# A two-layer encoder on one core: order of the activation sums behind the norm's row, order of the weight sums ahead of their split, sizes of two small tiles

## The chip, the cores and the metric

One NeuronCore of a Trainium2 chip runs the whole network. The time is device microseconds of one execution, the median of several. A profile of one execution lists every instruction of the five engines (TensorE for matmuls, VectorE and ScalarE for elementwise work, GpSimd, and SyncE, which issues the loads) with its start, its duration and what it waited for.

## The reference

Two layers over 256 tokens of width 2048, in float32. Layer 0 mixes with pooling and grouped-query attention, layer 1 with an mLSTM matrix memory. After each mixer comes a gated feed-forward, which is where this change acts:

```python
def conv_ffn(x, w_up, conv_w, conv_b, w_down):
    u = x @ w_up
    up = jnp.pad(u, ((0, 0), (1, 1), (0, 0)))
    c = conv_w.astype(u.dtype)
    u = c[0] * up[:, :-2] + c[1] * up[:, 1:-1] + c[2] * up[:, 2:] + conv_b.astype(u.dtype)
    gate, val = jnp.split(u, 2, axis=-1)
    return (jax.nn.silu(gate) * val) @ w_down
...
        x = x + mixed
        x = x + conv_ffn(rms_norm(x, norm_ffn[layer]), w_up[layer], conv_w[layer], conv_b[layer], w_down[layer])
```

The width of the gate and of the value is 5632 each. `rms_norm` divides each token's row by its root mean square and multiplies by a gain per column.

## The kernel before

**Products in two parts.** Float32 weights and activations are split into a high part of a shorter format and the remainder; a product is high x high + high x low + low x high, three passes through TensorE. The activations after a norm are the tile `xx` (high and low), scaled by the gain but not by the token's factor, which is multiplied on after the matmul.

**The stream of weights.** All weights come in chunks of 128 x 1024 float32, 512 KB, in the order of their use. `Stream.load` (L81) lets SyncE load a chunk into a `w` buffer (six, and one more in the feed-forward, from the pool `fw`). `Stream.split` (L93) makes the high part on ScalarE (L105) and the remainder on VectorE (L106) into an `hl` buffer (four, and one more in the feed-forward, from the pool `fh`). `Stream.next` (L120) hands the chunk to the matmuls after keeping loads up to seven and splits up to three chunks ahead, in the feed-forward. Some chunks carry a `kind`: for "sum" the right half gets the left half added (L99); for "chain" the left half first gets the right half of the last "sum" chunk added (L102), and then the right half gets the left (L103). A "sum" chunk's buffer is thus read until the "chain" chunk that follows it has been added.

**The feed-forward.** `_ffn_plan` writes out the order of steps: six groups of 4 or 8 column tiles; `up` computes a tile of gate and of value from 4 chunks, `down` multiplies finished groups by `w_down`. In two groups, four tiles are computed by `quads` instead: a block product with seven instead of eight multiplications, which needs sums of blocks of the activations (`sx`, made by `sums`, L930) and of the weights (the "sum" and "chain" chunks). `UNITS` says between which groups of the plan the chunks of a quad are strewn; there are 28 chunks for each of two quads in each of two layers. Each quad makes seven products `p` per pair of blocks; the first half of `sx` serves the first four pairs, the second half the last four.

**The row of the norm.** `Norm.finish` (L294) adds up the squares (L298), takes the inverse root (`rsqrt`, L224 to L231, with one power on GpSimd, L226) and gets a column `rcol` of factors. For norms 1 and 3, the ones ahead of the feed-forwards, it then makes two diagonal matrices `dg` (L310), multiplies them by ones on TensorE (tile `npr`, L313), and copies the product out as the row R (L315). `n0` (L1085) is minus `rcol`.

**What sets the order.** TensorE runs in the order of the program. The program itself is woven: generators such as `Norm.finish`, `sums_ready` and `quads`' `finish` are queued with a delay in estimated microseconds (`Weave.add`), and each step of the stream of matmuls advances that clock (`Weave.tick`) and lets at most one task go on. `Weave.until` runs tasks until something is there; the first `up` asks with it for R (L925). Within this order, the instructions of VectorE, ScalarE, GpSimd and SyncE are put in order by a list scheduler that plays the program through with estimated durations and takes, when an engine is free, the earliest instruction of the program that is ready. It can therefore put an instruction far ahead of its place in the program. On the chip each engine then works strictly in the order so found. `tc.keep_in_program_order(ins)` adds an edge, for order alone, from the last instruction traced on the same engine before `ins`: the scheduler may not put `ins` ahead of that one.

Of the kernel before, what the change touches and what calls it, by code (L numbers as in the profile page):

```python
# [9 lines left out]
F32 = mybir.dt.float32  # L10
# [6 lines left out]
P = 128  # L17
# [47 lines left out]
class Stream:  # L65


    def __init__(self, nc, wpool, spool, srcs, load_ahead, split_ahead):
        self.nc, self.wpool, self.spool, self.srcs = nc, wpool, spool, srcs
        self.la, self.sa = load_ahead, split_ahead  # L70
        self.w, self.hl = {}, {}
        self.n_load = self.n_split = self.at = 0
        self.more = None
# [7 lines left out]
    def load(self, pieces=1):  # L81
        i = self.n_load
        src = self.srcs[i]
        kind, src = src if isinstance(src, tuple) else ("plain", src)
        width = src.shape[-1]
        n = width // pieces
        w = self.home(i, True).tile([P, CH * P], F32, tag="w", name=f"w{i}")
        for c in range(0, width, n):
            self.nc.sync.dma_start(w[:, c : c + n], src[:, c : c + n])
        self.w[i] = w, n, width, kind  # L90
        self.n_load += 1

    def split(self, then=None):  # L93
        i = self.n_split
        w, n, width, kind = self.w.pop(i)
        hl = self.home(i, False).tile([P, 2, CH * P], F32R, tag="hl", name=f"hl{i}")
        l, r = w[:, 0:512], w[:, 512:1024]
        if kind == "sum":
            self.nc.vector.tensor_add(r, r, l)  # L99
            self.sum = r  # L100
        if kind == "chain":
            self.nc.vector.tensor_add(l, l, self.sum)  # L102
            self.nc.vector.tensor_add(r, r, l)  # L103
        for c in range(0, width, n):
            (self.nc.vector.tensor_copy if i + c == 0 else self.nc.scalar.copy)(hl[:, 0, c : c + n], w[:, c : c + n])  # L105
            self.nc.vector.tensor_sub(hl[:, 1, c : c + n], w[:, c : c + n], hl[:, 0, c : c + n].bitcast(F32))  # L106
            then and then(c // n)
        self.hl[i] = hl
        self.n_split += 1

    def ahead(self, i, split=None):
        n = len(self.srcs)
# [14 lines left out]
class Weave:  # L127
# [6 lines left out]
    def add(self, gen, delay=0.0):  # L134
        self.q.append([self.t + delay, gen])
# [37 lines left out]
def trunk(ctx: ExitStack, tc: tile.TileContext, gx, xT, xn, call, catt, cml, weights, out):  # L173
    nc = tc.nc
    v, a, g, pe = nc.vector, nc.scalar, nc.gpsimd, nc.tensor
# [7 lines left out]
    wp = pool("wraw", 6)  # L183
    sp = pool("wsplit", 4)
    smp = pool("small", 2)
    sm1 = pool("small1", 1)
# [5 lines left out]
    gcol = cp.tile([P, NG], F32, tag="gcol", name="gcol")  # L192
    a_x = actp.tile([P, KT, S], F32, tag="B1", name="xT")
    x = xp.tile([P, 2, D], F32, tag="x", name="x")
    st = Stream(nc, wp, sp, weights, 5, 2)

    gx0 = actp.tile([P, NG + 2 * S], F32, tag="B0", name="gx0")
    ctx.enter_context(tc.manual_schedule(engines={mybir.EngineType.PE}))
# [11 lines left out]
    wv = Weave()  # L210
# [34 lines left out]
    class Norm:  # L245
# [48 lines left out]
        def finish(self):  # L294
            n = self.n
            yield from wv.wait(lambda: self.blocks == NB)
            s2 = smp.tile([P, 2], F32, tag="nsum", name=f"nsum{n}")
            v.tensor_reduce(s2, self.ss, AX.X, ALU.add)  # L298
            self.rcol = rsqrt(s2, 2, 1.0 / D, f"n{n}")
            yield 2.5  # L300
            if n % 2 == 0:
                rr = dram.tile([2, P], F32, tag="rr", name=f"rr{n}")
                g.dma_start(rr.rearrange("t p -> p t"), self.rcol)
                R = sm1.tile([P, S], F32, tag="R", name=f"R{n}")
                g.dma_start(R.rearrange("p (t q) -> p t q", t=2), rr.unsqueeze(0).to_broadcast([P, 2, P]))
                self.R = R
                return
            dg = sm1.tile([P, 2, P], F32, tag="dg", name=f"dg{n}")
            for t in range(2):
                v.tensor_scalar_mul(dg[:, t, :], ident, self.rcol[:, t : t + 1])  # L310
            yield 1.0
            pr = psp.tile([P, 512], F32, tag="ps", name=f"npr{n}")
            mm(pr[:, 0:S], ones, dg.rearrange("p a b -> p (a b)"), True, True)  # L313
            R = sm1.tile([P, S], F32, tag="R", name=f"R{n}")
            v.tensor_copy(R, pr[:, 0:S])  # L315
            self.R = R
# [571 lines left out]
    def ffn_layer(layer, norm, nxt):  # L888
        with ExitStack() as es:
# [4 lines left out]
            xsp = cp1 = lp(f"fs{layer}", 1)  # L894
# [35 lines left out]
            def sums():  # L930

                vv = actp.tile([P, 2, KT // 2, S], F32, tag="B1", name=f"v{layer}")
                for h in range(2):
                    ks = slice(8 * h, 8 * h + 8)
                    v.tensor_add(vv[:, 0], norm.xx[:, ks, 0, :].bitcast(F32), norm.xx[:, ks, 1, :].bitcast(F32))
                    yield 5.0
                    q = vv[:, 0].rearrange("p (a k) (t c) -> p a k t c", k=2, t=2)
                    a11, a21, a12, a22 = (q[:, :, k, t, :] for k in range(2) for t in range(2))
                    raw = vv[:, 1].rearrange("p k s -> p (k s)").rearrange("p (j a c) -> p j a c", j=4, a=4)
                    s1, s2, s3, s4 = (raw[:, j] for j in range(4))  # L940
                    v.tensor_sub(s1, a21, a22)
                    v.tensor_add(s3, a11, a21)
                    yield 3.0
                    v.scalar_tensor_tensor(s2, s1, -1.0, a11, ALU.mult, ALU.subtract)
                    v.tensor_sub(s4, s3, a12)
                    v.tensor_sub(s4, s4, a22)
                    yield 4.0
                    for j in range(4):
                        hi, lo = (sx[:, j, 4 * h : 4 * h + 4, i, :] for i in range(2))
                        a.copy(hi, raw[:, j])  # L950
                        v.tensor_sub(lo, raw[:, j], hi.bitcast(F32))
                        yield 2.0
# [15 lines left out]
            def quads(fs, gt, i0, name):  # L968
# [8 lines left out]
                r0, r1 = norm.rcol[:, 0:1], norm.rcol[:, 1:2]  # L977
                for p in range(m):
                    ends = p == 0, p == m - 1
                    hl = st.next()  # L980
                    if p == 0:
                        b1, b5 = bank(1), bank(5)
                    product(b1, block_of(2 * p, 0), hl, 0, *ends)
                    product(b5, sum_of(0, p), hl, 512, *ends)
                    yield
                    hl = st.next()
                    if p == 0:
                        b6, b4 = bank(6), bank(4)
                    product(b6, sum_of(1, p), hl, 0, *ends)
                    product(b4, block_of(2 * p + 1, 1), hl, 512, *ends)  # L990
                    if p == m - 1:
                        c12, c21, c22 = part(12), part(21), part(22)
                        a.activation(c12, b1, AF.Copy, scale=n0)
                        a.activation(c21, b1, AF.Copy, scale=r1)
                        a.activation(c22, b5, AF.Copy, scale=r1)
                        v.scalar_tensor_tensor(c12, b6, n0, c12, ALU.mult, ALU.add)
                    yield
# [21 lines left out]
            def finish(top, bottom, fs, gt, i0, name):  # L1019

                for n, f in enumerate(fs):
                    tr = psp.tile([P, 2, S], F32, tag="ps", name=f"tr{layer}_{f}")
                    for j in range(2):
                        for t, src in enumerate((top, bottom)):
                            c = (2 * j + n) * P
                            pe.transpose(tr[:, j, t * P : t * P + P], src[:, c : c + P], ident)
                    u = tp.tile([P, 2, S], F32, tag="tb", name=f"tb_{layer}_{f}")
                    a.copy(u, tr)
                    tail(u, f, gt, i0 + n)
                    yield 2.5  # L1030

            def down_end(gt, b, kts):

# [44 lines left out]
            wv.add(norm.finish(), 4.0)  # L1078
            sx = xsp.tile([P, 4, KT // 2, 2, P], F32R, tag="sx", name=f"sx{layer}")

            n0 = xsp.tile([P, 1], F32, tag="n0", name=f"n0_{layer}")

            def sums_ready():
                yield from wv.wait(lambda: norm.R is not None)
                v.tensor_scalar_mul(n0, norm.rcol[:, 0:1], -1.0)  # L1085
                yield from sums()

            wv.add(sums_ready(), 8.0)
            st.la, st.sa, st.more = 7, 3, (lp(f"fw{layer}", 1), lp(f"fh{layer}", 1), st.at + len(_ffn_plan()))
            gts, run = {}, {}  # L1090
            for step in _ffn_plan():
                kind, c = step[:2]
                if kind != "d" and c not in gts:
# [78 lines left out]
    return np.concatenate(out)  # L1172


UNITS = {2: (1, 3), 4: (3, 5)}


def _ffn_plan():

    slots, begin = [], []  # L1180
# [9 lines left out]
    begin.append(len(slots))  # L1190
    here = [[] for _ in slots]
    m = KT // 2
    for c, (c0, c1) in UNITS.items():
        lo, hi = begin[c0] + 2, begin[c1] - 7
        one, two = 2 * m, m + m // 2
        step = (hi - lo - 3) / (one + two)
        for k in range(one + two):
            here[int(lo + k * step + (3 if k >= one else 0))].append(("s", c, 0))
# [148 lines left out]
```

## Time and profile before

| | us |
|---|---|
| median of 3 runs | 2224.29 |
| runs | 2223.16, 2224.29, 2226.46 |
| the profiled execution | 2224.29 |
| its span, first to last instruction | 2222.0 |
| TensorE busy | 2193.0 |
| VectorE busy | 1668.8 |
| ScalarE busy | 1228.3 |
| mean granted TensorE clock | 0.995 of full |

A row of the profile names a line of the kernel, an engine, an operation, the tile that it writes and those that it reads (`hl<-w,hl`), the form, and how often it occurs. "PE" is TensorE's matmuls, "PEld" its weight loads, "DVE" VectorE, "ACT" ScalarE, "POOL" GpSimd, "SPq" SyncE's queue of loads. What follows `<-` in square brackets is what ended the idle time before the instruction. The line L219 is a helper that issues all matmuls, so that they are told apart by their tiles: `up` and `dn` of the feed-forward, `p` of the quads, `npr` of the norm's row. In the timeline, instructions of one kind that follow each other are merged into one row.

### The profile page before, as it was taken

The page shows a single profiled execution, that of the slowest core. Times are in us where ns is not written, and L with a number is a line of the kernel's source. Part 1 is how long each engine was busy: PE and PEld are TensorE (multiplying, and loading weights), DVE is VectorE, ACT ScalarE, POOL GpSimd, SP SyncE. Part 2 cuts the span into 40 slices and gives each one's busy share as a digit, 9 for nine tenths or more (in the row PEclk, how much of TensorE's full clock was granted, in tenths as well). Part 3 has the DMA queues.
Part 4 walks back from the last instruction along what each step waited for, and adds up shares of the span by engine and source line. Part 5 has one row for each costly group of instructions (what it writes and reads, how often), then busy time and mean ns, then how long its engine had stood idle before and what let it go on. Part 6 is the DMA issues. An engine that isn't in the chain of part 4 may idle for free.

```text
span 2222.0 us, 30399 instructions
## 1 busy us (share of the span) xinstructions
PE 2193.0 (99%) x11328; PEld 1864.8 (84%) x11328; DVE 1668.8 (75%) x2378; ACT 1228.3 (55%) x1744; POOL 28.1 (1%) x40
## 2 busy tenths in 40 slices
PE   9999899999999999999999999989999999999999
PEld 7888688888888888889888888868888888888887
DVE  7686778788787787666767666677878878778764
ACT  7675555556555565556555455545555655556552
POOL 0020000000000000000000000000000000000000
PEclk9999999999999999999999999999999999999999
DMA  8545546676666766556555555645667666676553
GB/s 317 187 157 181 170 164 215 209 239 215 217 221 222 222 198 191 188 157 206 163 193 184 185 180 167 198 162 165 213 210 238 217 215 220 223 223 199 190 190 123
DMA packets 124951, 440.88 MB, mean 198 GB/s; under 512 B 13851, under 2 KB 16195, under 8 KB 124803
## 3 DMA queue, kind: packets, MB, share of 16 engines
q1 hardware_dynamic: 121568, 434.93, 59.8%
q10 hardware_dynamic: 3074, 3.75, 0.7%
q8 instruction: 89, 1.46, 0.3%
q0 software_dynamic: 160, 0.26, 0.1%
q14 instruction: 60, 0.48, 0.1%
HBM read 436.74 MB, written 2.14 MB: 198 GB/s over the span
## 4 chain that ended last, share of the span: by engine, by line
PE 85%; DVE 6%; DMA 6%; issue 2%; ACT 0%; DVEq 0%; ACTq 0%
PE up L219 27%; PE dn L219 20%; PE op L219 8%; DMA w<-in_q 6%; PE p L219 5%; PE mv L219 4%; PE mq L219 4%; PE mk L219 4%; PE mo L219 4%; DVE hl L106 3%; PE qproj L219 3%; PE kproj L219 1%; PE pool L219 1%; PE vproj L219 1%; PE qk L219 1%
## 5 line engine op out<-in xcount | busy, mean ns | idle before, releaser
L106 DVE TENSOR_TENSOR hl<-w,hl 128x1024 fp32r<-128x1024 f32 (+1 forms) x820 | 992.3, 1217 | 295.8 <-ACT hl L105 291.7
L105 ACT CAST hl<-w 128x1024 fp32r<-128x1024 f32 (+1 forms) x819 | 851.7, 1047 | 570.6 <-PE up L219 185.5
L219 PE MATMUL up<-xx,hl 128*128 128x512 f32 (+1 forms) x4608 | 829.7, 338 | 1.9 <-DVE hl L106 1.9
L219 PEld LDWEIGHTS up<-xx,hl 128*128 128x128 f32 x4608 | 719.5, 189 | 114.6 <-DVE hl L106 4.8
L219 PE MATMUL dn<-hl,g 128*128 128x512 f32 x2064 | 485.0, 391 | 0.6 <-DVE hl L106 0.6
L219 PEld LDWEIGHTS dn<-hl,g 128*128 128x128 f32 x2064 | 385.2, 188 | 83.2 <-DVE hl L106 1.2
L908 ACT ACTIVATE y<-tb_up,cst 128x256 f32<-128x256 f32 x144 | 78.8, 595 | 84.6 <-DVE tb_up L927 83.5
L219 PE MATMUL p<-hl,sx 128*128 128x512 f32 x384 | 104.2, 393 | 0.0
L99 DVE TENSOR_TENSOR w<-w 128x512 f32<-128x512 f32 x64 | 44.3, 692 | 76.4 <-DMA w<-in_q 76.2
L382 ACT COPY tb_up<-up 128x512 f32<-128x512 f32 x72 | 42.2, 586 | 102.6 <-PE up L219 100.3
L219 PE MATMUL mk<-xx,hl 128*128 128x512 f32 (+1 forms) x512 | 92.2, 337 | 0.0
L219 PE MATMUL mq<-xx,hl 128*128 128x512 f32 (+1 forms) x512 | 92.1, 337 | 0.0
L219 PE MATMUL mv<-hl,xx 128*128 128x512 f32 (+2 forms) x480 | 91.7, 350 | 0.0
L219 PE MATMUL op<-hl,cat 128*128 128x512 f32 x384 | 91.6, 393 | 0.0
L219 PE MATMUL mo<-hl,xx 128*128 128x512 f32 x384 | 90.4, 391 | 0.0
L219 PE MATMUL op<-hl,mcat 128*128 128x512 f32 x384 | 89.5, 392 | 0.0
L219 PEld LDWEIGHTS mq<-xx,hl 128*128 128x128 f32 x512 | 79.2, 188 | 11.6
L219 PEld LDWEIGHTS mk<-xx,hl 128*128 128x128 f32 x512 | 79.0, 188 | 11.4
L219 PEld LDWEIGHTS mv<-hl,xx 128*128 128x128 f32 x480 | 78.3, 189 | 11.2
L219 PEld LDWEIGHTS op<-hl,mcat 128*128 128x128 f32 x384 | 71.5, 188 | 14.6
L219 PEld LDWEIGHTS mo<-hl,xx 128*128 128x128 f32 x384 | 71.0, 188 | 14.1
L219 PEld LDWEIGHTS op<-hl,cat 128*128 128x128 f32 x384 | 70.9, 188 | 14.1
(240 smaller groups left out, 1746.9 us busy)
## 6 DMA issues: line engine op xcount, KB each, us to landing
w<-in_up SPq DMA_DIRECT2D x288, 512.0 KB, 4.1
w<-in_dn SPq DMA_DIRECT2D x176, 512.0 KB, 4.3
w<-in_m_in SPq DMA_DIRECT2D x124, 512.0 KB, 4.1
w<-in_q SPq DMA_DIRECT2D x112, 512.0 KB, 4.2
w<-in_a_in SPq DMA_DIRECT2D x46, 512.0 KB, 4.3
w<-in_a_out SPq DMA_DIRECT2D x32, 512.0 KB, 3.4
w<-in_m_out SPq DMA_DIRECT2D x32, 512.0 KB, 3.5
w<-in_m_g SPq DMA_DIRECT2D x5, 432.0 KB, 3.5
```

The lines of the kernel that those rows point to most:

```text
L99: self.nc.vector.tensor_add(r, r, l)
L105: (self.nc.vector.tensor_copy if i + c == 0 else self.nc.scalar.copy)(hl[:, 0, c : c + n], w[:, c : c + n])
L106: self.nc.vector.tensor_sub(hl[:, 1, c : c + n], w[:, c : c + n], hl[:, 0, c : c + n].bitcast(F32))
L219: pe.matmul(out_, lhsT, rhs, start=start, stop=stop, skip_group_check=True)
L382: a.copy(tb, ps[:, :, 1, :])
L908: a.activation(y[:, j, :], u[:, j, :], AF.Identity, scale=cw(tl, 1), bias=cw(tl, 3))
```

## The change

The sums of activations (L935, in each of two halves) and the sums of weights are pinned with `keep_in_program_order`. The weight sums move out of `split` into a function `sums`, called for chunk i + 1 at the end of the split of chunk i (and for chunk i at the start of its own, if that hasn't happened). The task that makes the activation sums is queued with a delay of 14 instead of 8. The tiles `dg` and `n0` are allocated larger, which puts the feed-forward's pools on multiples of 256 bytes. A second quad of a layer now asks that the first's `finish` tasks be done (`late`). `UNITS` spells out offsets that were written in `_ffn_plan`, with the same values.

```diff
-        self.w[i] = w, n, width, kind
+        self.w[i] = [w, n, width, kind, False]
         self.n_load += 1
+
+    def sums(self, i):
+        if i in self.w and not self.w[i][4] and self.w[i][3] != "plain":
+            w, kind = self.w[i][0], self.w[i][3]
+            l, r = w[:, 0:512], w[:, 512:1024]
+            pin, add = self.tc.keep_in_program_order, self.nc.vector.tensor_add
+            if kind == "sum":
+                pin(add(r, r, l))
+                self.sum = r
+            if kind == "chain":
+                pin(add(l, l, self.sum))
+                pin(add(r, r, l))
+            self.w[i][4] = True
 
     def split(self, then=None):
         i = self.n_split
-        w, n, width, kind = self.w.pop(i)
+        self.sums(i)
+        w, n, width = self.w.pop(i)[:3]
         hl = self.home(i, False).tile([P, 2, CH * P], F32R, tag="hl", name=f"hl{i}")
-        l, r = w[:, 0:512], w[:, 512:1024]
-        if kind == "sum":
-            self.nc.vector.tensor_add(r, r, l)
-            self.sum = r
-        if kind == "chain":
-            self.nc.vector.tensor_add(l, l, self.sum)
-            self.nc.vector.tensor_add(r, r, l)
...
         self.hl[i] = hl
         self.n_split += 1
+        self.sums(i + 1)
...
-            dg = sm1.tile([P, 2, P], F32, tag="dg", name=f"dg{n}")
+            dg = sm1.tile([P, 2 * P + 16], F32, tag="dg", name=f"dg{n}")[:, : 2 * P]
+            dg = dg.rearrange("p (t q) -> p t q", t=2)
...
-                    v.tensor_add(vv[:, 0], norm.xx[:, ks, 0, :].bitcast(F32), norm.xx[:, ks, 1, :].bitcast(F32))
+                    tc.keep_in_program_order(
+                        v.tensor_add(vv[:, 0], norm.xx[:, ks, 0, :].bitcast(F32), norm.xx[:, ks, 1, :].bitcast(F32)))
...
+                    if p == 0:
+                        wv.until(lambda: not late)
+                        late.update((0, 2))
...
+                late.discard((i0 - 4) % 4)
...
-            n0 = xsp.tile([P, 1], F32, tag="n0", name=f"n0_{layer}")
+            n0 = xsp.tile([P, 64], F32, tag="n0", name=f"n0_{layer}")[:, 0:1]
...
-            wv.add(sums_ready(), 8.0)
+            wv.add(sums_ready(), 14.0)
...
-UNITS = {2: (1, 3), 4: (3, 5)}
+UNITS = {2: (1, 2, 3, -7), 4: (3, 2, 5, -7)}
...
-    for c, (c0, c1) in UNITS.items():
-        lo, hi = begin[c0] + 2, begin[c1] - 7
+    for c, (c0, d0, c1, d1) in UNITS.items():
+        lo, hi = begin[c0] + d0, begin[c1] + d1
```

More of the change, by code (lines that the diff above doesn't have):

```diff
@@ L65, with __init__ @@
 class Stream:
-    def __init__(self, nc, wpool, spool, srcs, load_ahead, split_ahead):
-        self.nc, self.wpool, self.spool, self.srcs = nc, wpool, spool, srcs
+    def __init__(self, tc, wpool, spool, srcs, load_ahead, split_ahead):
+        self.tc, self.nc, self.wpool, self.spool, self.srcs = tc, tc.nc, wpool, spool, srcs
         self.la, self.sa = load_ahead, split_ahead
@@ L194, in trunk @@
     x = xp.tile([P, 2, D], F32, tag="x", name="x")
-    st = Stream(nc, wp, sp, weights, 5, 2)
+    st = Stream(tc, wp, sp, weights, 5, 2)
     gx0 = actp.tile([P, NG + 2 * S], F32, tag="B0", name="gx0")
@@ L1086, in sums_ready @@
                 yield from sums()
-            wv.add(sums_ready(), 8.0)
+            wv.add(sums_ready(), 14.0)
             st.la, st.sa, st.more = 7, 3, (lp(f"fw{layer}", 1), lp(f"fh{layer}", 1), st.at + len(_ffn_plan()))
-            gts, run = {}, {}
+            gts, run, late = {}, {}, set()
             for step in _ffn_plan():
```

## The prediction

> **What bounds the kernel now.** I read the page's first line and busy shares first.
>
> ```profile
> span 2222.0 us, 30399 instructions
> ...
> PE 2193.0 (99%) x11328; PEld 1864.8 (84%) x11328; DVE 1668.8 (75%) x2378; ACT 1228.3 (55%) x1744; POOL 28.1 (1%) x40
> ```
>
> TensorE is busy 2193.0 of 2222.0 us. No matmul is added or removed, so the change can win only TensorE's idle time, about 29 us, and time in which its matmuls run slower than elsewhere. What ends the idle time is in the view of waits, for matmuls (PE) and weight loads (PEld): total us, number, longest.
>
> ```profile
> PE npr L219 <- DVE n L1085: 21.3, 2, 10.7
> ...
> PEld up L219 <- DVE hl L106: 4.8, 7, 1.2
> PEld dn L219 <- DVE hl L106: 1.2, 2, 0.7
> ```
>
> Nearly all of it is two waits of 10.7 us, one in each feed-forward, for the matmul `npr` that spreads the norm's factors into the row R. The name L1085 (n0) is an accident of order: it ends beside `dg` (L310), which `npr` reads. The rest are small waits for a split chunk (L106), 6.0 us at the weight loads. In the timeline (start, us, what) VectorE around the first of the two, a cast of ScalarE, then TensorE:
>
> ```profile
> 257.18 2.28 DVE L935 TENSOR_TENSOR v<-xx 128x2048 f32<-128x2048 f32 x1
> 259.38 1.22 DVE L106 TENSOR_TENSOR hl<-w,hl 128x1024 fp32r<-128x1024 f32 x1
> 260.52 0.15 DVE L298 TENSOR_REDUCE nsum<-nss 128x2 f32<-128x8 f32 x1
> ...
> 270.59 2.29 DVE L935 TENSOR_TENSOR v<-xx 128x2048 f32<-128x2048 f32 x1
> 272.79 0.68 DVE L951 TENSOR_TENSOR sx<-v,sx 128x512 fp32r<-128x512 f32 x1
> 273.39 0.16 DVE L230 TENSOR_SCALAR re_n<-re_n 128x2 f32<-128x2 f32 x1
> ...
> 275.94 0.48 DVE L310 TENSOR_SCALAR dg<-cst,re_n 128x128 f32<-128x128 f32 x2
> ...
> 265.24 1.05 ACT L105 CAST hl<-w 128x1024 fp32r<-128x1024 f32 x1
> ...
> 260.76 5.14 PE L219 MATMUL up<-xx,hl 128*128 128x512 f32 x28
> 276.56 1.19 PE L219 MATMUL npr<-dg,cst 128*128 128x256 f32 x2 [10.66 <-DVE n L1085]
> ```
>
> The norm's chain is six instructions of 0.15 us on VectorE (L298, L224, L228 to L231), one on GpSimd and two for `dg`, yet L298 to L310 takes 15.4 us: into each gap the scheduler has put a piece of the activation sums (L935 to L951), which could run as soon as their blocks of xx were there. TensorE is through at 260.76 + 5.14 = 265.90 and stands until 276.56.
>
> **Part 1, L935 pinned behind n0.** n0 reads the norm's factor, so L935, and with it every later step of the sums, moves behind the chain. Each L935 gives back 2.2 us (270.59 to 272.79, start to next start), each 512-wide piece 0.6 (272.79 to 273.39). Ahead of `dg` stand two L935 and 13 such pieces (L941, L942, L944 and L945 twice, L946 once, L951 four times): 2 x 2.2 + 13 x 0.6 = 12.2 us. Without them `dg` starts at 275.94 - 12.2 = 263.7 and `npr` could go at 264.3, before TensorE needs it at 265.9. What could still hold it is a split: two L106 of 1.22 us let in ahead of `dg` make `npr` 266.7, a stall of 0.8. The worst that I see is the split of the cast at 265.24: it is ready at 266.3, ends at 267.5, then come L229 to L231, `dg` and the 0.6 from `dg` to `npr`, 269.2 in all, a stall of 3.3. So the two stalls of 21.3 leave between 0 and 6.6. I take 0.5 each, nearer to the sum that ends 1.6 us early: **-20.3**.
>
> What runs after the stall is slower too. Windows of TensorE: width, busy, granted clock, DMA share, GB/s; then TensorE's timeline.
>
> ```profile
> 277.00:281.00 4.00, 4.00 (x14) 0.53 0.00 0
> ...
> 1497.00:1501.00 4.00, 4.00 (x12) 0.50 0.00 0
> 1501.00:1505.00 4.00, 4.00 (x21) 0.79 0.00 0
> ...
> 277.19 45.91 PE L219 MATMUL up<-xx,hl 128*128 128x512 f32 x252
> 322.94 0.87 PE L219 MATMUL p<-hl,xx 128*128 128x512 f32 x3
> ...
> 851.70 22.46 PE L219 MATMUL up<-xx,hl 128*128 128x512 f32 x128
> 873.99 11.12 PE L219 MATMUL dn<-hl,g 128*128 128x512 f32 x48
> ...
> 1497.47 46.65 PE L219 MATMUL up<-xx,hl 128*128 128x512 f32 x252
> 1543.96 0.86 PE L219 MATMUL p<-hl,xx 128*128 128x512 f32 x3
> ```
>
> The granted clock is 0.53 and 0.50 in the 4 us after the stalls. In a stretch with no disturbance 128 matmuls of `up` take 873.99 - 851.70 = 22.29, 174.1 ns each; 252 should take 43.9. After the stalls they took 45.75 and 46.49: 1.9 and 2.6 lost. With no stall: **-4.5**; with one long enough to bring the clock down: 0.
>
> The Trainium skill, page "TensorE: Matmul & The Clock Gate", section "Part 1: The HAM clock gate (the "warmup" mystery)", says that an idle window of about 3.4 us halves TensorE's clock, and that as much sustained work restores it. The trace agrees: 0.53 and 0.50, full again some 4 to 8 us later. By that rule a stall merely cut to 4 us would keep the whole 4.5; by the row alone the loss could shrink with the stall.
>
> **Part 2, what the sums now collide with.** They are not gone. By line and form (count, busy us, mean ns), both feed-forwards together:
>
> ```profile
> L951 DVE TENSOR_TENSOR sx<-v,sx 128x512 fp32r<-128x512 f32 x16 | 10.6, 680 | 0.0
> L935 DVE TENSOR_TENSOR v<-xx 128x2048 f32<-128x2048 f32 x4 | 9.1, 2283 | 0.0
> L945 DVE TENSOR_TENSOR v<-v 128x512 f32<-128x512 f32 x4 | 2.7, 683 | 0.0
> ...
> 256.00:277.00 21.00, 10.34 (x61) 9.04 (x60) 21.00 (x36) 11.36 (x19) 0.71 (x1) 0.85 0.38 127
> 277.00:323.00 46.00, 46.00 (x255) 39.99 (x255) 36.40 (x55) 26.09 (x36) 0.00 (x0) 0.96 0.47 157
> ...
> 323.00:534.00 211.00, 172.43 (x228) 1.00 0.67 222
> ...
> 323.00:534.00 211.00, 107.18 (x91) 1.00 0.67 222
> ```
>
> Five lines like L945 make 13.5, so 33.2 in all, 16.6 us a layer. The windows give PE, PEld, DVE, ACT, POOL; the third DVE alone, the last L106 alone (91 splits in 211 us, one in 2.3). VectorE works 21.00 + 36.40 = 57.4 us between 256 and 323, and without stall and clock loss that stretch shrinks from 67 to 54.4. It cannot hold everything. But the first product with a sum comes at its end, and the half of the sums that it needs (8.3 us) fits: 57.4 - 8.3 = 49.1 of 54.4. The other half is read from the ninth quad chunk on, some 60 us later, where VectorE has 211 - 172.4 = 38.6 us free. I take **0**. The bound if the free time can't be used, since VectorE works in order: 16.6 less the 46 - 36.4 = 9.6 that are free in the first stretch, 7 us a layer, 14 in all. ScalarE's casts of the sums (L950) move along; it is half idle in both windows. Moving the task's start from 8 to 14 only lowers its rank behind the splits. What stands behind a delayed L935 is the copy of R (L315), which the first tail needs only after the first `up` group; so 0.
>
> **Part 3, weight sums one chunk ahead of their split.** The count stays (64 of L99, 32 each of L102 and L103). The groups of these adds by line (count, busy us, mean ns, idle before and what ended it), the page's row of these loads (count, size, us to landing), and the place where it hurts most:
>
> ```profile
> L99 DVE TENSOR_TENSOR w<-w 128x512 f32<-128x512 f32 x64 | 44.3, 692 | 76.4 <-DMA w<-in_q 76.2
> ...
> L102 DVE TENSOR_TENSOR w<-w,w 128x512 f32<-128x512 f32 x32 | 22.1, 691 | 36.2 <-DMA w<-in_q 35.9
> ...
> w<-in_q SPq DMA_DIRECT2D x112, 512.0 KB, 4.2
> ...
> 1619.54 0.33 SPq L89 DMA_DIRECT2D w<-in_q  x1
> 1623.78 0.69 DVE L102 TENSOR_TENSOR w<-w,w 128x512 f32<-128x512 f32 x1 [3.13 <-DMA w<-in_q]
> 1625.59 1.22 DVE L106 TENSOR_TENSOR hl<-w,hl 128x1024 fp32r<-128x1024 f32 x1
> ...
> 1626.86 5.39 PE L219 MATMUL up<-xx,hl 128*128 128x256 f32 x30 [0.81 <-DVE hl L106]
> ```
>
> VectorE stood 76.2 + 35.9 = 112 us for chunks that hadn't landed; behind the one at 1623.78 waited the split that TensorE wanted. Pinned behind the split of the chunk before it, a sum meets data loaded several splits earlier, and these waits end. That can win at most the 6.0 us at the weight loads; 0 if other VectorE work makes the same splits late. I take two thirds, as the worst of them is of this kind: **-4**. The new cost: ScalarE's cast of a quad chunk now starts after VectorE's previous split and the sum, so VectorE can wait for that cast: 1.05 us at each of 112 / 4 = 28 quad chunks of a stretch, 29.4 us, with the 8.3 from part 2 37.7 of the 38.6 free if no tail is put into the holes. Tight, but 0; what goes beyond is in rival (b). SyncE: the w buffer of a "sum" chunk is held until the "chain" chunk's add, some two splits longer than now, and SyncE's queue stands behind it; loads are issued seven buffers ahead, so 0, and the price without that lead is the slower rival.
>
> **Part 4, the rest.** Rounding `dg` and `n0` up shifts the feed-forward's buffers; splits in them now take what others take, and nothing is timed by a load's landing: 0, bounds -1 and +1. `UNITS` spells out the same starts and ends; `late` waits for transposes that are traced long before the second quads begin: 0.
>
> **The sum.** The profiled execution took 2224.29 us (2.3 around its span) and is itself the median of the three. 2224.3 - 20.3 - 4.5 - 4 = **2195.5**; with the bounds on the good side (21.3, 4.5, 6.0, 1) 2191.5.
>
> **Rivals.**
> (a) *The row still comes late.* Splits and L285 fill the gaps of the chain instead of the sums; 3.3 us remain at each, the clock still falls: 14.7 + 0 + 4 = 18.7, **2205.6**. For it: four L106 stood in that window. Against: they come up at TensorE's pace, not all at once.
> (b) *VectorE becomes the bound.* The 14 us of part 2 are paid, at the first products: **2209.5**. For it: 100% busy in the first window, and 37.7 of 38.6 above. Against: over half of that, 12.2, is the sums themselves, and 112 us of waits are freed.
> (c) *Slower: loads come late.* Where a chain chunk's add holds the sum chunk's buffer, SyncE's queue stands, and the held loads land after TensorE has used up its split chunks. The longest wait of TensorE for a split is now 1.2 us; at each of the 32 chain chunks (L102) that is 38.4, against 20.3 + 4.5 won: 2224.3 + 13.6 = **2237.9**. It decides once the lead of a load falls below the 4.2 us to landing plus cast and split, 6.5 us; seven buffers of 2.3 us less two leave 11.5.
> (d) *It doesn't do what it says.* L935 is ordered only behind n0; if pieces of the chain other than the sums set its pace, nothing but part 3 is won: **2220.3**.
>
> **How the numbers follow.** Forecast 0.66 (2190 to 2201, from the bounds), (a) 0.13, (b) 0.11, (c) 0.06, (d) 0.04. The range 2190 to 2211 holds the forecast and rivals (a) and (b), so leaves out 0.10 and the tails of these. A measurement tells about 0.2%, 4.4 us, from no change: faster 0.90, same 0.04, slower 0.06.
>
> **What would show it.** No row "npr <- DVE" of over 1 us; L935 after L1085 in time; granted clock 1.00 in the first 50 us of each feed-forward and 252 matmuls of `up` in 43.9 us; no "w <- DMA w<-in_q" among VectorE's waits; PEld's "hl L106" under 2 us. It is wrong if TensorE waits for `sx`, if "hl L106" grows past 10 us, or if SyncE's loads of the quads land after the cast that wants them.

## The result, and the profile after

| | before | after |
|---|---|---|
| median of the runs side by side, us | 2225.38 (2223.16 to 2227.27) | 2188.64 (2188.49 to 2188.67) |
| ratio, with 95% interval | | 0.9838 (0.9824 to 0.9851) |
| span of the profiled execution, us | 2222.0 | 2186.3 |

Faster, as forecast, but by more: 2188.64 against 2195.5, and below the range's low end of 2190. The profiled spans differ by 35.7 us; the forecast was 28.8. First the page's head, then two views of the changed kernel: the waits of TensorE and its weight loads for splits, with VectorE's longest (total us, number, longest), and the timeline of VectorE and TensorE around the norm's row of layer 0. The lines of the kernel have moved on: L113 is the split, L945 the first step of the activation sums, L1099 `n0`, L319 `dg`, L227 the helper of the matmuls.

```profile
span 2186.3 us, 30347 instructions
...
PE 2180.1 (100%) x11328; PEld 1861.1 (85%) x11328; DVE 1673.3 (77%) x2378; ACT 1229.4 (56%) x1744; POOL 29.2 (1%) x40
```

```profile
DVE hl L113 <- ACT hl L112: 350.8, 340, 2.6
...
PEld p L227 <- DVE hl L113: 1.7, 2, 0.8
...
PE p L227 <- DVE hl L113: 1.1, 2, 0.5
```

```profile
258.60 0.16 DVE L306 TENSOR_REDUCE nsum<-nss 128x2 f32<-128x8 f32 x1
...
259.99 1.23 DVE L113 TENSOR_TENSOR hl<-w,hl 128x1024 fp32r<-128x1024 f32 x1
...
262.63 0.47 DVE L319 TENSOR_SCALAR dg<-cst,re_n 128x128 f32<-128x128 f32 x2
263.02 0.15 DVE L1099 TENSOR_SCALAR n<-re_n 128x1 f32<-128x1 f32 x1
263.08 2.28 DVE L945 TENSOR_TENSOR v<-xx 128x2048 f32<-128x2048 f32 x1
...
296.65 2.29 DVE L945 TENSOR_TENSOR v<-xx 128x2048 f32<-128x2048 f32 x1
...
260.91 5.15 PE L227 MATMUL up<-xx,hl 128*128 128x512 f32 x28
265.89 0.60 PE L227 MATMUL npr<-dg,cst 128*128 128x256 f32 x2
266.14 44.24 PE L227 MATMUL up<-xx,hl 128*128 128x512 f32 x252
310.22 0.85 PE L227 MATMUL p<-hl,xx 128*128 128x512 f32 x3
```

The chain from L306 to L319 now takes 4.0 us instead of 15.4, the first L945 starts right behind `n0`, and `npr` starts at 265.89 with no wait at all. The 252 matmuls of `up` behind it take 310.22 - 266.14 = 44.1 us. VectorE has no row "w <- DMA w<-in_q" left; what has grown is its wait for the casts, from 291.7 to 350.8 us. TensorE's weight loads have two waits for splits left, 1.7 us in sum. Every sign that the prediction named is there, and the time is still 6.9 us lower.

Both programs issue the same 11328 matmuls in the same order, so each can be compared with itself: the time from its start to the next one's start, before minus after. Summed by place:

| where | us | forecast |
|---|---|---|
| the two waits for `npr`, 10.82 each | 21.6 | 20.3 |
| the slow steps right behind them, 1.96 + 2.55 | 4.5 | 4.5 |
| waits for late splits, 1.66 + 3.20, less a new wait at the second quad chunk, 0.80 + 0.79 | 3.3 | 4 |
| thousands of steps that are a few ns shorter, no stall among them | 6.2 | 0 |

That is 35.6 of the 35.7. Three terms are within 1.3 us of the forecast; the second had to come out, since forecast and table both take it from the trace of before. The fourth is the surprise: 3.5 us of it lie in the 2064 matmuls of `dn`, 2.2 in the 672 of `p`, 0.6 in the 4608 of `up`. One row before and the same row after, from the groups by line and form (count, busy us, mean ns, idle before):

```profile
L219 PE MATMUL dn<-hl,g 128*128 128x512 f32 x2064 | 485.0, 391 | 0.6 <-DVE hl L106 0.6
```

```profile
L227 PE MATMUL dn<-hl,g 128*128 128x512 f32 x2064 | 480.9, 390 | 0.0
```

A stretch with no disturbance, in the timeline after:

```profile
857.86 11.05 PE L227 MATMUL dn<-hl,g 128*128 128x512 f32 x48
868.75 22.45 PE L227 MATMUL up<-xx,hl 128*128 128x512 f32 x128
```

Its 48 matmuls, four chunks, take 868.75 - 857.86 = 10.89 us. The same 48 before, in the rows of the prediction, took 884.95 - 873.99 = 10.96, the next start being that of this row of before:

```profile
884.95 22.46 PE L219 MATMUL up<-xx,hl 128*128 128x512 f32 x128
```

0.07 us in 48 is 1.5 ns each on the mean, and the steps sorted by chunk say where it lies. In the feed-forward five `hl` buffers go round. Before, the step of `dn` is 227 ns in four of them and 233.4 ns in the fifth, the one from the pool `fh`; after, it is 227 in all five. 12 matmuls of a chunk by 6.4 ns make the 0.07. The first few matmuls behind a chunk of the fifth buffer are slow too (230, 236, 228, 233 and 231 ns in many of them, then 227): of the 3.5 us of `dn`, 2.4 lie in the fifth buffer's own 372 matmuls.

### The profile page after: what moved, and what is told of

It reads as the page before. It is cut to its first block, busy times and chain, and to the rows that moved or that the text cites. A ratio compares the mean times of both kernels' runs of the same rounds, so it can differ in the third digit from the quotient of the medians.

```text
span 2186.3 us, 30347 instructions
## 1 busy us (share of the span) xinstructions
PE 2180.1 (100%) x11328; PEld 1861.1 (85%) x11328; DVE 1673.3 (77%) x2378; ACT 1229.4 (56%) x1744; POOL 29.2 (1%) x40
## 4 chain that ended last, share of the span: by engine, by line
PE 97%; DVE 2%; issue 0%; ACT 0%
PE up L227 34%; PE dn L227 21%; PE op L227 8%; PE p L227 7%; PE mv L227 4%; PE mq L227 4%; PE mk L227 4%; PE mo L227 4%; PE qproj L227 3%; PE pool L227 1%; PE kproj L227 1%; PE vproj L227 1%; DVE hl L113 1%; PE av L227 1%; PE qk L227 1%; PE end L227 0%
## 5 line engine op out<-in xcount | busy, mean ns | idle before, releaser
L113 DVE TENSOR_TENSOR hl<-w,hl 128x1024 fp32r<-128x1024 f32 (+1 forms) x820 | 992.6, 1218 | 357.6 <-ACT hl L112 350.8
L227 PE MATMUL up<-xx,hl 128*128 128x512 f32 (+1 forms) x4608 | 823.1, 337 | 0.0
L227 PEld LDWEIGHTS up<-xx,hl 128*128 128x128 f32 x4608 | 716.1, 188 | 109.1
L227 PE MATMUL dn<-hl,g 128*128 128x512 f32 x2064 | 480.9, 390 | 0.0
L227 PEld LDWEIGHTS dn<-hl,g 128*128 128x128 f32 x2064 | 385.0, 188 | 78.5
L227 PE MATMUL p<-hl,sx 128*128 128x512 f32 x384 | 103.5, 391 | 1.1 <-DVE hl L113 1.1
L227 PE MATMUL mk<-xx,hl 128*128 128x512 f32 (+1 forms) x512 | 92.2, 338 | 0.0
L227 PE MATMUL mq<-xx,hl 128*128 128x512 f32 (+1 forms) x512 | 92.2, 337 | 0.0
L227 PE MATMUL mv<-hl,xx 128*128 128x512 f32 (+2 forms) x480 | 91.7, 350 | 0.0
L227 PE MATMUL op<-hl,cat 128*128 128x512 f32 x384 | 91.6, 393 | 0.0
L227 PE MATMUL mo<-hl,xx 128*128 128x512 f32 x384 | 90.5, 391 | 0.0
L227 PE MATMUL op<-hl,mcat 128*128 128x512 f32 x384 | 89.5, 392 | 0.0
L227 PEld LDWEIGHTS mq<-xx,hl 128*128 128x128 f32 x512 | 79.3, 188 | 11.6
L227 PEld LDWEIGHTS mk<-xx,hl 128*128 128x128 f32 x512 | 79.1, 188 | 11.4
L227 PEld LDWEIGHTS mv<-hl,xx 128*128 128x128 f32 x480 | 78.3, 189 | 11.2
L392 DVE TENSOR_TENSOR tb_up<-up,tb_up 128x512 f32<-128x512 f32 x72 | 49.8, 692 | 47.7 <-ACT tb_up L391 47.6
L227 PEld LDWEIGHTS op<-hl,mcat 128*128 128x128 f32 x384 | 71.5, 188 | 14.6
L227 PEld LDWEIGHTS mo<-hl,xx 128*128 128x128 f32 x384 | 71.0, 188 | 14.3
L227 PEld LDWEIGHTS op<-hl,cat 128*128 128x128 f32 x384 | 70.9, 188 | 14.1
```

What stands on the lines that cost most here:

```text
L227: pe.matmul(out_, lhsT, rhs, start=start, stop=stop, skip_group_check=True)
L392: v.tensor_add(tb, ps[:, :, 0, :], tb)
```

## The experiments

What the fourth row comes from was the question. Theory A: the start addresses. `dg` grows by 64 bytes a partition and `n0` from 4 bytes, which take up 32, to 256; all that is allocated behind them moves. In the built programs `sx` starts 192 bytes behind a multiple of 256 before, and the buffers from `fw` and `fh` 224 behind one; after, all three start on a multiple. The other `w` and `hl` buffers and the tiles of activations are on multiples in both. Theory B, the rival: the steps are shorter for another reason in the change, and the sizes do nothing.

The first four kernels take the change apart: undo the sizes, or make one part alone on top of before.

**The sizes undone, on after:**

```diff
-            dg = sm1.tile([P, 2 * P + 16], F32, tag="dg", name=f"dg{n}")[:, : 2 * P]
-            dg = dg.rearrange("p (t q) -> p t q", t=2)
+            dg = sm1.tile([P, 2, P], F32, tag="dg", name=f"dg{n}")
...
-            n0 = xsp.tile([P, 64], F32, tag="n0", name=f"n0_{layer}")[:, 0:1]
+            n0 = xsp.tile([P, 1], F32, tag="n0", name=f"n0_{layer}")
```

> The changed kernel with the sizes of dg and n0 undone; the order on every engine stays. Theory A (the extra 6 us come from where the buffers lie: matmuls that read sx or the fifth hl buffer off a multiple of 64 bytes take 3 to 6 ns longer): 2188.6 + 6.2 = 2194.8 us, dn matmuls on every fifth chunk 233 ns apart instead of 227, the two long waits for npr stay away. Rival B (matmuls are faster because the new order of VectorE and the loads collides less with TensorE's reads): 2188.6 us, all dn matmuls 227 ns apart.

Measured 2194.70 (2194.61 to 2194.79), 6.1 above after. `dn` is back at its sum of before, but for the late splits:

```profile
L227 PE MATMUL dn<-hl,g 128*128 128x512 f32 x2064 | 484.5, 391 | 0.0
```

Its step is 233.4 ns in the fifth buffer and 227 in the others again. The order of instructions on every engine is the same as in after, here and in the other kernels that only move buffers, so that the addresses alone differ. Theory A holds; and without this term the forecast of 2195.5 is 0.8 off.

**The sizes alone, on before** (the two tiles enlarged, nothing else of the change):

> The kernel before with the larger dg and n0 alone; its order stays. Theory A: 2224.8 - 6.2 = 2218.6 us, both waits of 10.7 us at npr still there, dn matmuls all 227 ns apart. Rival B: no change, 2224.8 us.

Measured 2220.29 (2217.76 to 2223.0), ratio 0.998 (0.997 to 0.999); the profiled span is 2215.5, 6.5 below that of before. The two waits of 10.7 us are still there:

```profile
PE npr L219 <- DVE n L1086: 21.3, 2, 10.7
```

By the span the sizes bring their 6 us here too, and the steps without a stall among them are 5.9 us shorter in sum. The medians say 5, but the runs of this kernel spread over 5 us themselves, so they alone would not size the term.

**The row alone, on before** (L935 pinned and the delay of 14; weight sums and sizes as before):

```diff
-                    v.tensor_add(vv[:, 0], norm.xx[:, ks, 0, :].bitcast(F32), norm.xx[:, ks, 1, :].bitcast(F32))
+                    tc.keep_in_program_order(
+                        v.tensor_add(vv[:, 0], norm.xx[:, ks, 0, :].bitcast(F32), norm.xx[:, ks, 1, :].bitcast(F32)))
...
-            wv.add(sums_ready(), 8.0)
+            wv.add(sums_ready(), 14.0)
```

> The kernel before with L935 pinned and the delay of 14, nothing else. Theory: both waits at npr and the slow clock behind them go, 21.6 + 4.5 = 26.1: 2198.7 us; the waits for chunks of q on VectorE stay, and the buffers stay off 64 bytes. Rival (the sums now collide with the splits, so that part is given back): above 2203 us, with PEld waiting for hl more than the 6.0 us of before.

Measured 2193.24 (2193.08 to 2193.49), 5.5 better than expected. Besides the 26.1 us of waits and slow steps, TensorE's 4.9 us of late splits are gone as well: of its waits only the one at the start of the program, for `wps`, is left. Yet VectorE stands for chunks that haven't landed as it did, if less:

```profile
DVE w L99 <- DMA w<-in_q: 51.5, 39, 3.2
...
DVE w L102 <- DMA w<-in_q: 16.9, 14, 2.4
```

So 68.4 us of VectorE's waits cost TensorE nothing here, where 112 went with 4.9 before.

**The weight sums alone, on before** (`Stream` as in the change):

> The kernel before with the weight sums pinned one chunk ahead of their split, nothing else. Theory: the waits of VectorE for chunks of q end and with them TensorE's waits for late splits: 4.9 less 1.6 for a new one, 3.3 us: 2221.5 us; npr still waits 2 x 10.7. Rival (loads late, since the buffer of a sum chunk is held longer): 2225 us or more, with casts waiting for loads.

Measured 2218.66 (2218.2 to 2219.88), ratio 0.9971 (0.9961 to 0.9981). The profiled span falls from 2222.0 to 2217.6, by 4.4; all late splits are gone, no new wait has come, and the two long ones are untouched:

```profile
PE npr L227 <- DVE n L1093: 21.3, 2, 10.7
PE wps L251 <- DVE pad L619: 1.2, 1, 1.2
```

The medians differ by 6.7 us, twice what was expected; TensorE's steps in the two traces account for the 4.4 of the span, and what the other runs of before lost beyond that wasn't traced.

The late splits can thus be ended by the row's pin or by the weight sums' pin, and they can be won only once.

The next kernels ask which buffer and which step of address it is. `dg` alone enlarged puts `sx` on a multiple and `fw` and `fh` 32 bytes behind one; `n0` alone leaves `sx`, `fw` and `fh` 192 behind.

**`dg` alone:**

```diff
-            n0 = xsp.tile([P, 64], F32, tag="n0", name=f"n0_{layer}")[:, 0:1]
+            n0 = xsp.tile([P, 1], F32, tag="n0", name=f"n0_{layer}")
```

> The changed kernel with n0 small again: sx starts on a multiple of 256 bytes, the fifth hl buffer 32 bytes past one. Theory A: p matmuls as in the changed kernel where hl is one of the other four (228 ns), every fifth dn chunk at 233: 2188.6 + 3.5 to 4.2 = 2192.5 us. Rival (sx alone matters): 2188.6 us. Rival B: 2188.6 us.

Measured 2195.12 (2194.99 to 2195.22): nothing won, 2.6 above what was expected. `dn` in the fifth buffer 233.5 ns. `p` is at 233.6 in the fifth buffer and still at some 230 in the other four, against 228 in after, although `sx` is on a multiple. So an offset of the fifth `hl` buffer alone keeps `p` slow too, and slows products that don't read it a little.

**`n0` alone:**

```diff
-            dg = sm1.tile([P, 2 * P + 16], F32, tag="dg", name=f"dg{n}")[:, : 2 * P]
-            dg = dg.rearrange("p (t q) -> p t q", t=2)
+            dg = sm1.tile([P, 2, P], F32, tag="dg", name=f"dg{n}")
```

> The changed kernel with dg small again: sx and the fifth hl buffer start 192 bytes past a multiple of 256, so on multiples of 64. Theory A with a step of 64 bytes: 2188.6 us, nothing lost. Theory A with a step of 256 bytes: 2194.8 us, as without both sizes.

Measured 2194.38 (2194.17 to 2194.44): 192 bytes, three times 64, is as bad. A multiple of 64 isn't enough.

**`hl` at 128 bytes** (`n0` as `[P, 32]`, so that `sx` stays on a multiple and `fw` and `fh` are 128 behind one):

> The changed kernel with n0 of 128 bytes: sx on a multiple of 256, the fifth hl buffer 128 bytes past one. Starts 32, 192 and 224 bytes past cost 6.4 ns for a 512-column read. If the step is 128 bytes: 2188.6 us, dn matmuls on every fifth chunk at 227 ns. If it is 256: 2194.5 us, 233 ns.

Measured 2194.68 (2194.56 to 2194.76), the fifth buffer's `dn` 232.9 ns. So a multiple of 32, 64 or 128 bytes isn't enough, and a multiple of 256 is.

**`sx` off, `hl` on** (`dg` as before, `n0` as `[P, 16]`: `sx` 192 behind, `fw` and `fh` on a multiple; the feed-forward's elementwise tiles `tb_up` and `y` move to 192 with `sx`):

> The changed kernel with dg as before and n0 of 64 bytes: sx 192 bytes past a multiple of 256, the fifth hl buffer on one. If the streamed operand alone carries the cost: 2188.6 us. If the loaded weights (sx) do too: some 1.4 ns at each of the 384 products with a sum, 0.5 us, at most 1 us more.

Measured 2190.51 (2190.45 to 2190.63), 1.9 above after. `sx` is the operand that is loaded as weights; the 384 products with it go from 103.5 to 104.6 us by the groups. But those with `xx` lose 0.4 us too, `up` 0.4 and `dn` 0.2, and neither operand of these is off a multiple. So an offset of `sx`, or of the tiles that move with it, slows its neighbours as well, and the start of a matmul's own operands isn't the whole account. The two offsets don't add up either: `hl` off 6.0, `sx` off 1.9, both 6.1. Part of the reason is that the size of the offset matters: `up`, where `hl` is the loaded operand, loses 2.0 us with `hl` at 128 and 0.7 at 224.

**Four `hl` buffers off** makes the suspected cost several times as large. On after, the four common buffers are put 32 bytes behind a multiple, and the tile behind them makes up for it, so that only these four leave their multiples (all that lies behind moves by 256):

```diff
+    pad = pool("pad0", 1).tile([P, 8], F32, tag="pad0", name="pad0")
...
+    pad = pool("pad1", 1).tile([P, 56], F32, tag="pad1", name="pad1")
```

> The changed kernel with the four common hl buffers moved to 32 bytes past a multiple of 256, the fifth and everything behind left on multiples of 256 (a 32-byte and a 224-byte tile that nothing reads are put around them). Theory A: matmuls that stream 512 columns of hl cost 6.4 ns more: in the feed-forwards 4/5 of 2784, elsewhere about 2070, 4300 in all, 27.5 us: 2216 us. Rival B, or an effect that belongs to one buffer: 2188.6 us.

Measured 2221.31 (2221.13 to 2221.88): 32.7 us lost, nearly the whole change, with no new wait and no clock lost. The timeline of the same stretch:

```profile
837.81 11.33 PE L229 MATMUL dn<-hl,g 128*128 128x512 f32 x48
848.97 22.61 PE L229 MATMUL up<-xx,hl 128*128 128x512 f32 x128
```

848.97 - 837.81 = 11.16 us for 48, 232.5 ns each, against 226.9 after. By step-to-step comparison `dn` loses 11.7 us, `up` 6.5, `p` 3.0, and the products of the mixers (`op`, `mo`, `mv`, `qproj` and others) most of the rest. The forecast of 2216 was 5 short, since it had priced only products that stream `hl`: in `up`, `hl` is loaded, and 4608 of these lose 1.4 ns each on the mean.

The last three kernels look at the order on VectorE.

**The delay back to 8, on after:**

```diff
-            wv.add(sums_ready(), 14.0)
+            wv.add(sums_ready(), 8.0)
```

> The changed kernel with the sums' task queued at 8 instead of 14. Theory: the pin alone frees the row, so no wait for npr over 1 us; the time within 1 us of 2188.6, and the wait of the second quad chunk (0.5 us a layer) no larger, since the second half of the sums is through sooner. Rival (the delay is what frees the row): a wait for npr of 5 us or more a layer, 2199 us or more.

Measured 2186.96 (2186.86 to 2187.06), 1.7 better than after, more than the 1 us that was expected: the new wait at the second quad chunk is gone. VectorE is nearly full there. Window 274 to 323 of after (width, busy of PE, PEld, DVE, ACT, POOL, granted clock, DMA share, GB/s) and its timeline:

```profile
274.00:323.00 49.00, 48.47 (x275) 41.91 (x274) 47.42 (x68) 32.19 (x46) 0.00 (x0) 1.00 0.58 182
...
311.08 0.69 DVE L102 TENSOR_TENSOR w<-w,w 128x512 f32<-128x512 f32 x1
...
313.07 0.69 DVE L103 TENSOR_TENSOR w<-w 128x512 f32<-128x512 f32 x1
...
314.81 0.69 DVE L99 TENSOR_TENSOR w<-w 128x512 f32<-128x512 f32 x1
...
316.80 3.49 DVE L113 TENSOR_TENSOR hl<-w,hl 128x1024 fp32r<-128x1024 f32 x3
...
318.08 0.74 PE L227 MATMUL p<-hl,sx 128*128 128x512 f32 x2 [0.53 <-DVE hl L113]
```

47.42 of 49 us busy, and a split comes 0.5 us late; ahead of it stand weight sums. With the late start of the sums or the early weight sums left out, in this kernel, the row alone and the next, there is no such wait. But how full VectorE is doesn't tell them apart: in the next kernel, which has no wait, the same window reads

```profile
274.00:323.00 49.00, 49.00 (x280) 42.64 (x280) 48.27 (x69) 31.00 (x43) 0.00 (x0) 1.00 0.62 201
```

So it is rather the order in which VectorE takes its work there that delays the split; which instruction of it does was not tried.

**The row and the sizes, without the weight sums** (on before: L935 pinned, delay 8, both tiles enlarged):

> The kernel before with L935 pinned and the larger dg and n0, the delay left at 8, the weight sums as they were. Theory (once the row is in time, the weight sums' pin wins nothing, and the wait of 0.7 us a layer at the second quad chunk needs both the delay of 14 and that pin): 2187.0 us, as the changed kernel with a delay of 8, though VectorE still waits some 70 us for chunks of q. Rival (the weight sums' pin is worth the 4.9 us that it wins alone): 2191 us or more, with PEld waiting for hl.

Measured 2186.90 (2186.77 to 2187.11), ratio to before 0.9831 (0.9813 to 0.9848). With the kernel just before it the best of all, and ahead of after by 1.7: once the row is in time the weight sums' pin wins nothing, although VectorE still stands for loads:

```profile
DVE w L99 <- DMA w<-in_q: 56.8, 40, 3.3
```

**Only the second half's L945 pinned, on after,** so that the first can run ahead of the row again and a shorter stall is left:

```diff
-                    tc.keep_in_program_order(
+                    (tc.keep_in_program_order if h else lambda ins: ins)(
```

> The changed kernel with the first half of the sums (L935, h = 0) not pinned. Theory: that half is back in the gaps of the norm's chain, npr waits the 10.7 us less one L935 and four pieces (2.2 + 2.4), 6.1 a layer; if any stall of this length brings the clock down as the long one did, 4.5 us on top: 2188.6 + 12.2 + 4.5 = 2205.3 us. Rival (the clock loss shrinks with the stall): 12.2 + 2.6: 2203.4 us. Rival (the pin does nothing for that half): 2188.6 us.

Measured 2204.18 (2203.97 to 2205.95). The stalls are down from 10.7 us to 6.3:

```profile
PE npr L227 <- DVE n L1099: 12.6, 2, 6.3
```

Windows of TensorE behind the stalls (width, busy, granted clock, DMA share, GB/s), of this kernel and then of before:

```profile
272.40:275.30 2.90, 2.90 (x8) 0.50 0.36 147
275.40:277.00 1.60, 1.60 (x11) 1.00 0.00 0
1483.60:1487.00 3.40, 3.40 (x10) 0.50 0.30 123
1487.10:1490.00 2.90, 2.90 (x18) 1.00 0.00 0
```

```profile
276.60:280.70 4.10, 4.10 (x12) 0.50 0.00 0
280.80:283.00 2.20, 2.20 (x14) 1.00 0.00 0
1496.90:1502.60 5.70, 5.70 (x17) 0.50 0.00 0
1502.80:1505.00 2.20, 2.20 (x15) 1.00 0.00 0
```

The granted clock falls as far, to 0.50, but is back sooner: 3.0 and 3.5 us after TensorE goes on, against 4.2 and 5.9 in before. The slow steps behind the two stalls lose 1.42 + 1.67 = 3.1 us, against 4.5. The new wait at the second quad chunk is half gone as well, 0.7 us for both layers together. The time is between the two expectations.

## Why the prediction was right and where it failed

**Part 1, the row: right.** Two L935 and 13 pieces did stand ahead of `dg`, and the pin moved them all behind it. The forecast left 0.5 us at each; nothing is left, and 21.6 instead of 20.3 came out. One split (259.99) and three short pieces of the norm's own work were let into the gaps of the chain in each layer, but `dg` started at 262.63, earlier than the 263.7 worked out, so they didn't matter. The clock's 4.5 is gone whole, and the half-pinned kernel shows what remaining stalls of 6.3 us would have kept: 3.1 of it. So the forecast's alternative, that a stall merely shortened keeps the whole 4.5, is not what happened. The clock stood at 0.50 for 3.0 and 3.5 us behind these stalls, and for 4.2 to 6.1 us behind the six stalls of 10.7 in the traces of before, of the sizes alone and of the weight sums alone. The Trainium skill, page "TensorE: Matmul & The Clock Gate", section "Part 1: The HAM clock gate (the "warmup" mystery)", halves the clock after an idle window of about 3.4 us and restores it after about 3.4 us of sustained work. The trace agrees on the half and, for the shorter stalls, on the time; behind the long ones the clock took longer. Whether a stall's length sets this or the moment at which it falls isn't shown: stalls of the same 10.7 us differ by 1.9 us.

**Part 2, the sums moved into the busy stretch: right in kind.** Cost 0 by the forecast, 14 at worst; 1.6 measured, at the second quad chunk, where VectorE is busy 97% of the window (and 99% in a kernel without the wait). It needs the delay of 14 together with the weight sums' pin, as three kernels without one of them show. "Moving the task's start from 8 to 14 only lowers its rank behind the splits" missed that.

**Part 3, the weight sums: right sum, wrong cause.** 4.9 of TensorE's late splits went, 3.3 net, against 4. But the working read VectorE's 112 us of waits for loads as their cause. Two kernels keep such waits, 68.4 us in the row alone, and have no late split. The row's pin alone ends them too. Why each of two quite different edits does it alone was not settled; the order of instructions on VectorE differs in each.

**Part 4, the sizes: this is the step that failed.** "Rounding `dg` and `n0` up shifts the feed-forward's buffers; splits in them now take what others take, and nothing is timed by a load's landing: 0, bounds -1 and +1." Splits and loads were looked at, and those don't change: L106 is 1.22 us in every buffer, and the feed-forward's loads land in 4.1 to 4.3 us before and 4.0 to 4.2 after. The reader of these buffers that bounds the kernel is TensorE, and it wasn't looked at. Its `dn` matmuls that stream from the buffer off a multiple of 256 bytes take 6.4 ns longer each, and the products `p`, the matmuls right behind and those that load weights from such a buffer lose a little too: 6.1 us in all, shown by undoing the sizes and six times the bound. Why TensorE is slower there stays open. It is what carried the time below the range. The steps of `dn` by buffer were in the trace of before, 227 and 233 ns, and sorting them by chunk would have shown it.

**The rivals.** (a), the row still late: refuted, `npr` doesn't wait. (b), VectorE the bound: at the right place, at 1.6 us instead of 14. (c), loads late: refuted; what holds VectorE now is the cast (350.8 us), and TensorE's weight loads wait for a split 0.8 us at most. (d), the change not doing what it says: refuted.

## What to carry to other kernels

Where TensorE is the bound, sort the step from one matmul's start to the next by the buffer that it reads: a few ns in and around one buffer of five are 6 us here, and a buffer's start is free to choose. Chains that TensorE waits for are worth a pin against work that is ready early but needed late; a pin on the first instruction of each half of that work was enough, and on the second half alone it left 6.3 us of 10.7. Two edits that cure the same stall are to be priced together: the second won nothing, and with the later start of the sums it cost 1.7.

## What the runs showed of the hardware that was not expected

- The step of `dn`, a 128x512 matmul, is 227 ns when the streamed operand's buffer starts on a multiple of 256 bytes a partition, and 233 when it starts 32, 128, 192 or 224 behind one. That is no rule for every matmul: the 512-column steps of `up`, which stream `xx` from a multiple, are 233 ns in after too. A loaded operand off costs 1.4 ns on the mean at each `up` with four `hl` buffers 32 behind, and about 3 at each `p` with `sx` 192 behind, in a kernel where elementwise tiles had moved too. VectorE's split and the landing of loads showed no such difference. What makes it so was not tried, nor why matmuls with both operands on a multiple lose a little as well, nor why the two offsets together cost less than their sum.
- Stalls cost twice: in the trace of before 10.7 us of idle time lost 2.0 and 2.5 us more through the clock, and 6.3 us lost 1.4 and 1.7.
- The late splits go with an uneven time, more than the long stalls do. The kernel before, with both, spread from 2222.0 to 2228.35 over 18 runs, and the sizes alone, with both, by 5.2 over ten. The weight sums alone, which keeps the stalls and has no late split, spread by 1.7 over nine, and the kernels without either by 0.2 to 0.8. In the traces of before and of the sizes alone, with the same order of work, different splits come late. What shifts them was not looked into.
